# Q/k/v projection columns in blocks of 512 across head groups, with changed prices in the planner that orders the instructions

## The chip, the cores and the metric

The kernel runs on one NeuronCore of a Trainium2 chip. The metric is the device time of one execution in microseconds (us). The engines are named as in the profile: PE is the matrix engine and PEld its weight loads, DVE the vector engine, ACT the scalar engine, POOL the general engine, SP the engine that issues all DMAs of this kernel.

## What is computed

Two decoder layers over 1024 positions of 1024 features, all in float32. Each layer normalizes, projects to queries, keys, values and a gate, attends, multiplies by silu(gate) and projects back onto the residual. Layer A has 16 query heads and 2 key heads with a window of 128. Layer B has three groups (dilations 1, 4, 16) of 16 query heads and 4 key heads, merged by their softmax denominators. Cut to the part around the change:

```python
def mixer_b(h, w_in, q_gain, k_gain, cos, sin):
    z = h @ w_in
    heads = z[..., :N_GROUPS * B_GROUP_COLS].reshape(b, s, N_GROUPS, B_GROUP_COLS)
    gate = z[..., N_GROUPS * B_GROUP_COLS:]
    for g, (window, dilation) in enumerate(B_PAIRS):
        q, k, v = jnp.split(heads[:, :, g], [nq, nq + nk], axis=-1)
        q = partial_rope(rmsnorm(q...), cos, sin)
        k = partial_rope(rmsnorm(k...), cos, sin)
        o, lse = dilated_group(q, k, v, window, dilation)
    ...
    return o * jax.nn.silu(gate)
```

## The kernel before

Matrix products keep float32 accuracy by splitting each operand into a high and a low part and issuing three matmuls (`mm3`, L500): high by high, high by low, low by high. `load_w` (L452) loads a weight block in eight slices of 128 rows and splits each on ACT (high) and DVE (low) into the tile `wt`; there are 12 such tiles, so one block of eight and half of the next. `proj_tile` (L505) multiplies one tile of 128 positions by such a block: 24 matmuls into the PSUM tile `psz`, which ACT copies to `z`. `bounce` (L709) does this for the eight position tiles and writes each `z` to DRAM (`za`, `zb`); `fetch` (L716) reads the rows back as `zi`, in the order that the dilation wants.

Layer A is done in four passes `n` of four query heads: columns 384, 256, 384, 256 (a pair of passes shares its key head, whose columns go with the first). Layer B has four passes `n`, and in each the groups `g` = 2, 1, 0, each with a block of 384 columns (256 of queries, 64 of keys, 64 of values). A block is projected, and then eight attention units follow, one for each 128 positions. A unit is `prep` (L548) and `attend` (L594): on PE first two transposes of `zi` into `pq`, then one of the keys `kk` (in layer A in every second pass only), then the scores `pss`, the transposed probabilities `ptt` and the output `po`; between them stand DVE and ACT steps (`qs`, `kring`, `pe`, `pp`, `oh`). `gate_block` (L523) computes the gate into `psg` once in a pass. After group 0 a merge (`merge_b`, L937) goes through DRAM with the factors (`cr` to `cd` to `cb`). The output projections go into `psw`.

The order in which the engines get their instructions is not the order of the code. Every call is recorded in `Plan` (L98) with its dependencies and with a price from `_price` (L299): how long it occupies its engine, and after how long its result is there. `forward` (L209) is a list scheduler over the five engines; `issue` (L283) runs it with the code's order, then eight rounds with priorities from a backward pass, and emits the order with the shortest planned end. On the chip each engine then works through its own list in order, and an instruction whose operand is late holds what is behind it. In the plan a DMA occupies SP for `ISSUE` (475 ns), its data starts 1100 ns later, and it has landed `TRIP` (1900 ns) after that.

In `prep` the queries are split in two halves of 64 partitions: for each half ACT writes the high part into `qs[:HD, :, two]`, and DVE the low part into `qs[HD:, :, two]`, which reads ACT's result. The two halves' columns alternate in `qs`, in runs of 128.

Of the kernel before, what the change touches and what calls it, by code (L numbers as in the profile page):

```python
# [12 lines left out]
F32 = mybir.dt.float32  # L13
# [5 lines left out]
P = 128  # L19
# [30 lines left out]
TRIP = 1900  # L50
# [3 lines left out]
YB = 0  # L54
NB = {"pz": 2, "pS": 2, "pT": 2, "pO": 1, "pM": 1}
# [42 lines left out]
class Plan:  # L98
# [12 lines left out]
    ISSUE = 475  # L111
# [97 lines left out]
    def forward(self, prio, users):  # L209
# [12 lines left out]
        while len(order) < n:  # L222
# [8 lines left out]
            if e == "SP":  # L231
                free[e] = s + self.ISSUE
                wait = max(0.0, dma - s - 1100)
                dma = max(dma, s + 1100) + occ
# [64 lines left out]
def _price(eng, name, out, ins, kw):  # L299

    n = out.free_size()
    if eng == "SP":
        t = out.size() * 4 / 300.0
        return t, t + 1100 + TRIP
# [5 lines left out]
    accum = kw.get("accum_out") is not None  # L310
    if eng == "ACT":
        t = 70 + 0.84 * n + (70 if held else 0) + (0 if ins[0].space == bass.MemoryType.PSUM else 65)
        return (t + 93, t + 73) if accum else (t, t + 90)
    if eng == "DVE":
        if name == "tensor_reduce":
            last = ins[0].ap[-1][0]
            t = 75 + (1.04 if last == 1 else 1.78) * ins[0].free_size()
        elif name == "reciprocal":
            t = 100 + 8 * n
        elif name == "tensor_scalar":  # L320
            t = 130 + 0.53 * n
        else:
            wide = 2.1 if steps and min(steps) >= 4 and n >= 2 * P else 1.04
            t = 70 + wide * n
            t += 80 if name in ("tensor_tensor_reduce", "scalar_tensor_tensor") else 0
        return t, t + 75
    if kw.get("op") is OP.pow:
        t = 270 + 172 * n
    elif n <= 8:
        t = 300  # L330
    else:
        t = 1.95 * n if n > 512 else (50 if 200 < n < 400 else 160) + 2.1 * n
# [24 lines left out]
def trunk(ctx, tc, x, norm_a, w_in_a, q_gain_a, k_gain_a, sinks_a, w_out_a,  # L357
# [147 lines left out]
    def proj_tile(hT, t, w, width, r=None):  # L505
# [5 lines left out]
        z = nc.tile(sp, [P, 384], F32, tag="z", bufs=3, name="z")  # L511
# [36 lines left out]
    def prep(kind, order, tpos, z, nh, kv, slot):  # L548
# [160 lines left out]
    def bounce(hT, w, width, name, r=None):  # L709
        zd = tc.dram_tile([T, width], F32, name=name)  # L710
        for t in range(NT):
# [14 lines left out]
    def w_a(n, big=None):  # L726
        return load_w(w_in_a, (0, 384, 640, 1024)[n], 256 if n % 2 else 384, 0, big=big)
# [32 lines left out]

    def w_b(g, n, ks=range(NK)):
        return load_w(w_in_b, g * GCOLS + n * 384, 384, 1, ks)
# [27 lines left out]
    def out_a_whole(ts):  # L790
# [9 lines left out]
        w = w_b(2, 0, range(4))  # L800
# [8 lines left out]
        return w + w_b(2, 0, range(4, NK))  # L809
# [3 lines left out]
    for n in range(4):  # L813
        w = w_a(n, None if n else nc.tile(sp, [P, 4, 512], F32, tag="v0", bufs=1, name="wbig"))
# [4 lines left out]
        if n == 0:  # L819
            zd = tc.dram_tile([T, width], F32, name="za0")  # L820
            for t in range(NT):
# [19 lines left out]
                z = proj_tile(hT, t, w, width, ra)  # L841
                nc.sync.dma_start(zd[t * P:(t + 1) * P], z[:, :width])
# [10 lines left out]
        else:  # L853
            zd = bounce(hT, w, width, f"za{n}", ra)
# [39 lines left out]
    w0 = out_a_whole((6, 7))  # L894
# [168 lines left out]
```

## Time and profile before

| | |
|---|---|
| median of 3 runs | 1289.74 us (1287.47 to 1290.97) |
| the profiled execution | 1286.87 us, its span 1285.0 us |
| PE, PEld | 97%, 88% of the span |
| DVE, ACT, POOL | 80%, 69%, 55% |
| matmuls | 7851, of them 3072 into `psz` |
| DMA | 149.74 MB, mean 117 GB/s |

The span is the profile's time from the first to the last instruction; about 1.9 us lie outside it. Busy time on PE contains the overlap of pipelined matmuls, so that a busy share of 97% does not say how much of it is waiting for the issue of the next; the distance of matmuls that follow each other without a gap tells that.

### The profile page before, as it was taken

How to read it: one execution, taken by the hardware profiler on the slowest of the kernel's cores; microseconds unless marked ns; L12 is line 12 of the kernel's file. 1: busy time of each engine (PE TensorE's matmuls, PEld its weight loads, DVE VectorE, ACT ScalarE, POOL GpSimd, SP SyncE). 2: the span in 40 equal slices, each digit the busy share in tenths (PEclk: the TensorE clock that was granted, in tenths of full speed). 3: DMA queues.
4: the chain of work that ended last, by engine and by line, in shares of the span. 5: the costliest groups of instructions: out<-in, count | busy, mean ns of one | idle time of the engine just before them, and what ended most of it. 6: DMA issues, size and time to landing. Idle time of an engine off the chain costs nothing. (4 is left out here: it accounts for less than half of the span.)

```text
span 1285.0 us, 25754 instructions
## 1 busy us (share of the span) xinstructions
PE 1244.5 (97%) x7851; PEld 1136.3 (88%) x7851; DVE 1028.3 (80%) x2968; ACT 880.5 (69%) x2377; POOL 708.3 (55%) x1388
## 2 busy tenths in 40 slices
PE   7999999999999999999999999999999999999998
PEld 6999899998688999989888999988999988998776
DVE  8668888777955428878888878889888989779896
ACT  5367686877733437877767887767887766987661
POOL 5655455455500038556567655477656567786632
PEclk9999999999999999999999999999999999999999
DMA  6423223245444233223233323244233244454525
GB/s 226 141 76 103 84 80 117 81 146 178 123 129 140 99 104 99 81 71 111 93 125 122 91 73 111 88 139 135 79 95 91 94 130 128 140 174 129 173 80 181
DMA packets 142666, 149.74 MB, mean 117 GB/s; under 512 B 33576, under 2 KB 129344, under 8 KB 142528
## 3 DMA queue, kind: packets, MB, share of 16 engines
q1 hardware_dynamic: 142528, 148.09, 36.7%
q8 instruction: 63, 1.03, 0.3%
q14 instruction: 75, 0.61, 0.2%
HBM read 105.57 MB, written 42.47 MB: 115 GB/s over the span
## 5 line engine op out<-in xcount | busy, mean ns | idle before, releaser
L352 PE MATMUL psz<-wt,hT 128*128 128x384 f32 (+1 forms) x3072 | 632.9, 343 | 5.7 <-DVE wt L352 2.8
L352 PEld LDWEIGHTS psz<-wt,hT 128*128 128x128 f32 x3072 | 510.8, 190 | 16.2 <-DVE wt L352 3.6
L352 PE MATMUL psg<-hT,wt 128*128 128x256 f32 x1536 | 220.3, 291 | 0.3 <-DVE gT L352 0.3
L352 PEld LDWEIGHTS psg<-hT,wt 128*128 128x128 f32 x1536 | 200.3, 191 | 2.3 <-PE psg L352 0.5
L352 ACT ACTIVATE pe<-pe,st 128x128 f32<-128x128 f32 (+1 forms) x384 | 169.1, 442 | 36.2 <-DVE st L352 33.7
L352 PE MATMUL ptt<-ident,pe 128*128 128x128 f32 x800 | 170.8, 275 | 2.8 <-ACT pe L352 2.6
L352 DVE SCALAR_TENSOR_TENSOR qs<-pq,gt,qs 64x256 fp32r<-64x256 f32 x256 | 123.9, 484 | 44.8 <-ACT qs L352 38.5
L352 DVE TENSOR_TENSOR pp<-ptt,pp 128x512 fp32r<-128x512 f32 x200 | 131.5, 684 | 32.2 <-ACT pp L352 30.6
L352 POOL TENSOR_TENSOR r<-r,ex 128x5 f32<-128x5 f32 (+1 forms) x128 | 150.6, 1176 | 5.6
L352 ACT ACTIVATE qs<-pq,gt 64x256 fp32r<-64x256 f32 x256 | 120.1, 469 | 42.9 <-PE pq L352 36.2
L352 DVE SCALAR_TENSOR_TENSOR wt<-raw,gt,wt 128x384 fp32r<-128x384 f32 (+1 forms) x188 | 114.5, 639 | 28.5 <-ACT wt L352 26.6
L352 ACT ACTIVATE pp<-ptt 128x512 fp32r<-128x512 f32 x200 | 111.9, 595 | 35.9 <-PE ptt L352 35.1
L352 ACT ACTIVATE oh<-po 64x512 f32<-64x512 f32 x128 | 76.0, 594 | 82.2 <-PE po L352 78.5
L352 DVE CUSTOM_DVE_ANT_0 pe<-pss,con,r 128x256 f32<-128x256 f32 x288 | 123.5, 477 | 8.9 <-PE pss L352 8.5
L352 PEld LDWEIGHTS ptt<-ident,pe 128*128 128x128 f32 x800 | 105.7, 140 | 21.8 <-ACT pe L352 9.8
L352 ACT ACTIVATE wt<-raw,gt 128x384 fp32r<-128x384 f32 (+1 forms) x188 | 98.9, 564 | 19.6 <-DMA raw<-in_w_in_b_dram 6.9
L352 PE MATMUL po<-pp,vring 128*128 128x512 f32 x280 | 106.9, 416 | 3.8 <-ACT pp L352 1.5
L352 POOL TENSOR_SCALAR r<-ss 128x5 f32<-128x5 f32 (+1 forms) x128 | 30.3, 237 | 144.7 <-DVE st L352 55.5
L352 PE MATMUL psw<-hT,wy 128*128 128x512 f32 x384 | 107.8, 408 | 2.0 <-ACT wy L352 1.2
L352 POOL TENSOR_TENSOR sq<-zi 128x320 f32<-128x320 f32 (+1 forms) x128 | 93.8, 733 | 25.3 <-DMA zi<-za 9.8
L352 PE MATMUL pss<-kring,qs 128*128 128x256 f32 x560 | 99.3, 286 | 2.5 <-DVE kring L352 2.3
L352 POOL TENSOR_TENSOR t<-zi,rg 128x80 f32<-128x80 f32 (+1 forms) x128 | 48.4, 378 | 93.3 <-DMA zi<-zb 60.2
(142 smaller groups left out, 2175.3 us busy)
## 6 DMA issues: line engine op xcount, KB each, us to landing
raw<-in_w_in_b_dram SPq DMA_DIRECT2D x96, 192.0 KB
zb<-z SPq DMA_DIRECT2D x96, 192.0 KB
cb<-cd SPq DMA_DIRECT2D x128, 128.0 KB
zi<-zb SPq DMA_DIRECT2D x64, 192.0 KB
raw<-in_w_in_a_dram SPq DMA_DIRECT2D x48, 128.0 KB
yraw<-yd SPq DMA_DIRECT2D x24, 256.0 KB
zi<-zb SPq DMA_DIRECT2D x64, 96.0 KB
xt<-in_xt_dram SPq DMA_DIRECT2D x16, 256.0 KB
```

What stands on the lines that cost most here:

```text
L352: self.plan.add(self.name, method, lambda: fn(*args, **kw), outs, ins, price, func)
```

## The change

- **Blocks of columns.** The weights of layer B are laid out on the host in the order in which the program uses them, and a new class `Bounce` cuts the q/k/v columns of a layer into blocks that no longer end with a head group: in layer A 512, 512, 256 in place of 384, 256, 384, 256, in layer B six blocks of 512 and then four of 384 in place of twelve of 384. A block's `z` is written to one DRAM tensor for each group that it touches, so with one or two DMAs. A call for a group projects blocks until that group is covered.
- **Prices.** `TRIP` goes from 1900 to 2900 ns, `ISSUE` from 475 to 520, and several DVE, ACT and POOL prices change.
- **Query split.** `qs` is laid out half by half, so that a half's columns are contiguous. Both ACT copies are recorded first, and both DVE subtractions are given a dependency on the second of them in the plan.

```diff
-TRIP = 1900
+LEAD = 1100
+TRIP = 2900
+CUTA = (512, 1024, 1280)
+CUTB = [512, 1024, 1536, 2048, 2560, 3072, 3456, 3840, 4224, 4608]
...
-    for g in range(3):
-        for n in range(4):
+    for n in range(4):
+        for g in (2, 1, 0):
...
-    ISSUE = 475
+    ISSUE = 520
...
     if eng == "ACT":
-        t = 70 + 0.84 * n + (70 if held else 0) + (0 if ins[0].space == bass.MemoryType.PSUM else 65)
-        return (t + 93, t + 73) if accum else (t, t + 90)
+        if accum:
+            return 342 + 0.625 * n, 284 + 0.84 * n
+        t = 70 + 0.84 * n + (70 if held else 0) + (0 if psum else min(75, 0.4 * n) + 25 * held)
+        return t, t + 90
...
+        elif n <= 16:
+            return 105, 215
         else:
-            wide = 2.1 if steps and min(steps) >= 4 and n >= 2 * P else 1.04
-            t = 70 + wide * n
-            t += 80 if name in ("tensor_tensor_reduce", "scalar_tensor_tensor") else 0
-        return t, t + 75
+            t = 70 + 1.04 * n
+            if name in ("tensor_tensor_reduce", "scalar_tensor_tensor"):
+                t += 60 if psum else 105
+            elif steps and min(steps) >= 4:
+                return (70 + 1.82 * n, 145 + 1.82 * n) if n >= 2 * P else (70 + 1.18 * n, 220 + 1.18 * n)
+        return t, t + 78
...
-        z = nc.tile(sp, [P, 384], F32, tag="z", bufs=3, name="z")
+        z = nc.tile(sp, [P, 512], F32, tag="z", bufs=3, name="z")
...
-        qs = nc.tile(sp, [P, 2, 2, P], F32R, tag="qs", bufs=2, name="qs")
+        qs = nc.tile(sp, [P, 2, 2, P], F32R, tag="qs", bufs=2, name="qs").rearrange("p two pr q -> p pr two q")
         gq = gc[:, 0, kind:kind + 1]
         for two in range(2):
             rows = slice(two * HD, two * HD + HD)
             nc.scalar.activation(qs[:HD, :, two], pm[rows, 0:2], AF.Copy, scale=gq[rows])
+        nc.after = {nc.last["ACT"]}
+        for two in range(2):
+            rows = slice(two * HD, two * HD + HD)
             nc.vector.scalar_tensor_tensor(qs[HD:, :, two], pm[rows, 0:2], gq[rows], f(qs[:HD, :, two]),
                                            op0=OP.mult, op1=OP.subtract)
+        nc.after = set()
...
+        def tile(self, hT, t, w, o, width, r):
             z = proj_tile(hT, t, w, width, r)
-            nc.sync.dma_start(zd[t * P:(t + 1) * P], z[:, :width])
-        return zd
+            for end, wd, zd in zip(self.ends, self.widths, self.zd):
+                a, b = max(o, end - wd), min(o + width, end)
+                if a < b:
+                    nc.sync.dma_start(zd[t * P:(t + 1) * P, a - end + wd:b - end + wd], z[:, a - o:b - o])
+
+        def blocks(self, i):
+            while self.done < self.ends[i]:
+                o, width = self.block()
+                if o not in self.weights:
+                    self.prefetch()
+                yield o, width, self.weights.pop(o)
+                self.done += width
+
+        def group(self, i, hT, r=None):
+            for o, width, w in self.blocks(i):
+                for t in range(NT):
+                    self.tile(hT, t, w, o, width, r)
+            return self.zd[i]
...
+    za = Bounce("za", (384, 256, 384, 256), CUTA, lambda o, width, big=None: load_w(w_in_a, o, width, 0, big=big))
+    zb = Bounce("zb", (384,) * 12, CUTB, lambda o, width, ks=range(NK): load_w(w_in_b, o, width, 1, ks))
...
-            zd = bounce(hT, w, width, f"za{n}", ra)
+            zd = za.group(n, hT, ra)
...
-            w = w0 if n == 0 and g == 2 else w_b(g, n)
-            zd = bounce(hT, w, 384, f"zb{g}_{n}")
+            zd = zb.group(3 * n + 2 - g, hT)
```

Three places in the order of the instructions. The first is PE at the start of layer B: `psz` is the first projected block, and the first `pq` is the first attention unit of the layer. Before:

```order
L352 MATMUL psz<-wt,hT 128x384 x9
L352 MATMUL pm<-ident,hn 128x128 x4
L352 MATMUL psz<-wt,hT 128x384 x173
L352 MATMUL pq<-ident,zi 128x128 x2
L352 MATMUL psz<-wt,hT 128x384 x12
L352 MATMUL pq<-ident,kk 128x128
L352 MATMUL psz<-wt,hT 128x384 x6
```

and now:

```order
L362 MATMUL psz<-wt,hT 128x512 x7
L362 MATMUL pm<-ident,hn 128x128 x4
L362 MATMUL psz<-wt,hT 128x512 x180
L362 MATMUL pq<-ident,zi 128x128 x2
L362 MATMUL psz<-wt,hT 128x512 x10
L362 MATMUL pq<-ident,kk 128x128
L362 MATMUL psz<-wt,hT 128x512 x5
```

About as many matmuls stand ahead of the first unit, but each has 512 columns in place of 384.

The second place is PE at the boundary of layer B's second and third pass, from the first transposes of the 49th unit of the layer on (the first of the third pass). Before:

```order
L352 MATMUL pss<-kring,qs 128x256 x7
L352 MATMUL pq<-ident,zi 128x128 x2
L352 MATMUL psz<-wt,hT 128x384 x5
L352 MATMUL ptt<-ident,pe 128x128 x2
L352 MATMUL psz<-wt,hT 128x384 x7
L352 MATMUL ptt<-ident,pe 128x128 x2
L352 MATMUL psz<-wt,hT 128x384 x4
L352 MATMUL ptt<-ident,pe 128x128 x2
L352 MATMUL psz<-wt,hT 128x384 x4
```

and now:

```order
L362 MATMUL pss<-kring,qs 128x256 x3
L362 MATMUL pq<-ident,zi 128x128 x2
L362 MATMUL pss<-kring,qs 128x256 x3
L362 MATMUL ptt<-ident,pe 128x128 x5
L362 MATMUL psg<-hT,wt 128x256 x25
L362 MATMUL pq<-ident,kk 128x128
L362 MATMUL po<-pp,vring 128x512
L362 MATMUL psg<-hT,wt 128x256 x4
L362 MATMUL po<-pp,vring 128x512
L362 MATMUL ptt<-ident,pe 128x128 x4
L362 MATMUL pss<-kring,qs 128x256 x4
```

The projection that stood between the steps of the units is gone from here; the gate of the second pass (`psg`) stands there, and some steps follow each other directly.

The third place is ACT in a unit of layer B, with the semaphores that an instruction waits for in brackets (names with DVE, PE or DMA in them are of those engines). Before:

```order
L352 ACTIVATE qs<-pq,gt 64x2x128 [waits PE_49]
L352 ACTIVATE pp<-ptt 128x512 [waits PE_49]
L352 ACTIVATE pp<-ptt 128x512 [waits PE_49,Activation_49]
L352 ACTIVATE qs<-pq,gt 64x2x128 [waits DVE_49]
L352 ACTIVATE wt<-raw,gt 128x384 [waits DMAHW2_49]
```

and now:

```order
L362 ACTIVATE pp<-ptt 128x512 [waits PE_49,Activation_49]
L362 ACTIVATE qs<-pq,gt 64x256 [waits PE_49]
L362 ACTIVATE qs<-pq,gt 64x256
L362 ACTIVATE vring<-zi 128x64 [waits DMAHW1_49,PE_49,Pool_49]
L362 ACTIVATE oh<-po 64x512 [waits PE_49,Activation_49]
```

The second query copy waited for DVE's subtraction in this unit (it does so in 16 of the 128 units); now the two copies come without a wait between them in every unit.

## Rows read from the trace of the kernel before

**Rows 1.** The page's first part: busy us, share of span, instructions

```profile
PE 1244.5 (97%) x7851; PEld 1136.3 (88%) x7851; DVE 1028.3 (80%) x2968; ACT 880.5 (69%) x2377; POOL 708.3 (55%) x1388
```

**Rows 2.** PE's groups by shape: count, busy us, mean ns, idle before and releasers

```profile
L352 PE MATMUL psz<-wt,hT 128*128 128x384 f32 x2688 | 577.3, 351 | 5.7 <-DVE wt L352 2.8 <-ACT wt L352 1.5 <-DVE qs L352 0.6
L352 PE MATMUL psg<-hT,wt 128*128 128x256 f32 x1536 | 220.3, 291 | 0.3 <-DVE gT L352 0.3
...
L352 PE MATMUL psw<-hT,wy 128*128 128x512 f32 x384 | 107.8, 408 | 2.0 <-ACT wy L352 1.2 <-DVE wx L352 0.8
```

**Rows 3.** Timeline of PE, long runs: start us, length us, what, idle before

```profile
55.06 5.88 PE L352 MATMUL psg<-hT,wt 128*128 128x256 f32 x47
...
440.61 0.60 PE L352 MATMUL pm<-ident,hn 128*128 128x128 f32 x4
...
445.11 25.21 PE L352 MATMUL psz<-wt,hT 128*128 128x384 f32 x144
...
1260.63 11.09 PE L352 MATMUL psw<-hT,wy 128*128 128x512 f32 x48
...
1275.35 5.95 PE L352 MATMUL psw<-hT,wy 128*128 128x512 f32 x24 [1.17 <-ACT wy L352]
```

**Rows 4.** Timeline of the start, DVE and then PE

```profile
11.01 2.77 DVE L352 SCALAR_TENSOR_TENSOR wt<-raw,gt,wt 128x384 fp32r<-128x384 f32 x2
13.71 1.14 DVE L352 SCALAR_TENSOR_TENSOR wt<-wbig,gt,wt 128x384 fp32r<-128x384 f32 x2
...
13.31 8.88 PE L352 MATMUL psz<-wt,hT 128*128 128x384 f32 x34 [2.42 <-DVE wt L352]
```

**Rows 5.** Windows: us, busy us of PE, PEld, DVE, ACT, POOL, clock, DMA, GB/s

```profile
0.00:32.00 32.00, 22.39 (x101) 20.74 (x101) 25.92 (x29) 16.46 (x29) 17.15 (x18) 1.00 0.67 227
...
475.20:1178.30 703.10, 689.24 (x4404) 639.10 (x4403) 604.28 (x1848) 540.82 (x1523) 460.91 (x939) 1.00 0.35 108
...
665.40:726.40 61.00, 59.21 (x416) 55.65 (x415) 55.62 (x177) 44.34 (x134) 43.17 (x84) 1.00 0.32 98
...
822.00:893.70 71.70, 68.46 (x438) 62.38 (x437) 65.40 (x201) 49.46 (x142) 50.52 (x89) 1.00 0.43 133
```

**Rows 6.** DVE's waits from 475.2 to 1178.3: us, times, longest

```profile
DVE qs L352 <- ACT qs L352: 23.9, 36, 2.2
DVE pp L352 <- ACT pp L352: 19.4, 26, 1.5
DVE pe L352 <- PE pss L352: 14.3, 30, 0.9
```

**Rows 7.** Waits of PE's weight loads, whole run: us, times, longest

```profile
PEld ptt L352 <- ACT pe L352: 9.8, 32, 1.0
PEld po L352 <- DVE pp L352: 8.0, 24, 1.0
...
PEld pss L352 <- DVE kring L352: 3.9, 8, 1.2
PEld pq L352 <- issue: 3.8, 12, 0.7
PEld pq L352 <- POOL r L352: 3.8, 4, 1.1
```

**Rows 8.** ACT's and DVE's groups by shape

```profile
L352 ACT ACT_TABLE_LOAD x29 | 37.2, 1283 | 1.2 <-PEq L1048 0.7
...
L352 DVE SCALAR_TENSOR_TENSOR wt<-raw,gt,wt 128x384 fp32r<-128x384 f32 x108 | 70.4, 680 | 20.4 <-ACT wt L352 19.3
L352 DVE SCALAR_TENSOR_TENSOR wt<-raw,gt,wt 128x256 fp32r<-128x256 f32 x80 | 44.2, 583 | 8.1 <-ACT wt L352 7.2
```

**Rows 9.** Waits for landed DMAs, and issues of the read-back (min/median/max ns)

```profile
POOL t L352 <- DMA zi<-zb: 60.2, 18, 33.9
...
L352 SPq DMA_DIRECT2D zi<-zb x128: 319/460/1489, 465.5 to 1214.9; - x128
```

More of the change, by code (lines that the diff above doesn't have):

```diff
@@ L232, in forward @@
                 free[e] = s + self.ISSUE
-                wait = max(0.0, dma - s - 1100)
-                dma = max(dma, s + 1100) + occ
+                wait = max(0.0, dma - s - LEAD)
+                dma = max(dma, s + LEAD) + occ
             else:
@@ L303, in _price @@
         t = out.size() * 4 / 300.0
-        return t, t + 1100 + TRIP
+        return t, t + LEAD + TRIP
     if eng == "PE":
@@ L310, in _price @@
     accum = kw.get("accum_out") is not None
+    psum = bool(ins) and ins[0].space == bass.MemoryType.PSUM
     if eng == "ACT":
-        t = 70 + 0.84 * n + (70 if held else 0) + (0 if ins[0].space == bass.MemoryType.PSUM else 65)
-        return (t + 93, t + 73) if accum else (t, t + 90)
+        if accum:
+            return 342 + 0.625 * n, 284 + 0.84 * n
+        t = 70 + 0.84 * n + (70 if held else 0) + (0 if psum else min(75, 0.4 * n) + 25 * held)
+        return t, t + 90
     if eng == "DVE":
         if name == "tensor_reduce":
-            last = ins[0].ap[-1][0]
-            t = 75 + (1.04 if last == 1 else 1.78) * ins[0].free_size()
-        elif name == "reciprocal":
+            t = 80 + (1.04 if ins[0].ap[-1][0] == 1 else 1.78) * ins[0].free_size()
+            return t, t + 65
+        if name == "reciprocal":
             t = 100 + 8 * n
@@ L321, in _price @@
             t = 130 + 0.53 * n
-        else:
-            wide = 2.1 if steps and min(steps) >= 4 and n >= 2 * P else 1.04
-            t = 70 + wide * n
-            t += 80 if name in ("tensor_tensor_reduce", "scalar_tensor_tensor") else 0
-        return t, t + 75
+        elif n <= 16:
+            return 105, 215
+        else:
+            t = 70 + 1.04 * n
[4 more added lines that the diff above has]
+        return t, t + 78
     if kw.get("op") is OP.pow:
         t = 270 + 172 * n
-    elif n <= 8:
-        t = 300
+    elif name == "tensor_scalar":
+        return 300 + 1.25 * n, 235 + 1.35 * n
     else:
@@ L707, in out_first, with __init__, block, prefetch @@
         nc.bias = 0
-    def bounce(hT, w, width, name, r=None):
-        zd = tc.dram_tile([T, width], F32, name=name)
-        for t in range(NT):
-            z = proj_tile(hT, t, w, width, r)
-            nc.sync.dma_start(zd[t * P:(t + 1) * P], z[:, :width])
-        return zd
+    class Bounce:
+        def __init__(self, name, widths, cuts, load):
+            self.ends = list(np.cumsum(widths))
+            self.widths = widths
+            self.zd = [tc.dram_tile([T, w], F32, name=f"{name}{i}") for i, w in enumerate(widths)]
+            self.load, self.done, self.cuts = load, 0, cuts
+            self.weights = {}
+        def block(self):
+            return self.done, next(c for c in self.cuts if c > self.done) - self.done
+        def prefetch(self, **kw):
+            o, width = self.block()
+            self.weights[o] = self.weights.get(o, []) + self.load(o, width, **kw)
+        def tile(self, hT, t, w, o, width, r):
+            z = proj_tile(hT, t, w, width, r)
+            for end, wd, zd in zip(self.ends, self.widths, self.zd):
[4 more added lines that the diff above has]
+            while self.done < self.ends[i]:
+                o, width = self.block()
+                if o not in self.weights:
[7 more added lines that the diff above has]
+            return self.zd[i]
     def fetch(zd, width, rows):
@@ L724, in trunk @@
     hB = {}
-    def w_a(n, big=None):
-        return load_w(w_in_a, (0, 384, 640, 1024)[n], 256 if n % 2 else 384, 0, big=big)
+    za = Bounce("za", (384, 256, 384, 256), CUTA, lambda o, width, big=None: load_w(w_in_a, o, width, 0, big=big))
+    zb = Bounce("zb", (384,) * 12, CUTB, lambda o, width, ks=range(NK): load_w(w_in_b, o, width, 1, ks))
     def put_w(raw, w, k, half, hi, lo, sub):
@@ L759, in load_wout_b @@
         nc.bias = 0
-    def w_b(g, n, ks=range(NK)):
-        return load_w(w_in_b, g * GCOLS + n * 384, 384, 1, ks)
     def halves(a):
@@ L799, in out_a_whole @@
             got.append((t, x1, ps))
-        w = w_b(2, 0, range(4))
+        zb.prefetch(ks=range(4))
         nc.bias = -SECB
@@ L808, in out_a_whole @@
         nc.bias = 0
-        return w + w_b(2, 0, range(4, NK))
+        zb.prefetch(ks=range(4, NK))
     wo = {}
@@ L813, in trunk @@
     for n in range(4):
-        w = w_a(n, None if n else nc.tile(sp, [P, 4, 512], F32, tag="v0", bufs=1, name="wbig"))
+        if n == 0:
+            za.prefetch(big=nc.tile(sp, [P, 4, 512], F32, tag="v0", bufs=1, name="wbig"))
         if n % 2 == 0:
@@ L819, in trunk @@
         if n == 0:
-            zd = tc.dram_tile([T, width], F32, name="za0")
+            zd = za.zd[0]
+            (o, zw, w), = za.blocks(0)
             for t in range(NT):
@@ L840, in trunk @@
                     late_constants()
-                z = proj_tile(hT, t, w, width, ra)
-                nc.sync.dma_start(zd[t * P:(t + 1) * P], z[:, :width])
+                za.tile(hT, t, w, o, zw, ra)
             pr = nc.tile(pM, [P, 4, P], F32, tag="m", bufs=NB["pM"], name="pr")
@@ L893, in trunk @@
         norm_pair(j, [parts[2 * j + i] for i in range(2)])
-    w0 = out_a_whole((6, 7))
+    out_a_whole((6, 7))
     hT = hB
```

## Prediction

> **What bounds the kernel now.** I read the shares of the engines first [rows 1]: PE 97%, DVE 80%, ACT 69%. Since matmuls overlap, the 97% says only that PE nearly always has something in flight; how long a matmul holds the next one up is read from long runs of one kind [rows 3]. There I take off the last matmul's own duration (the means in [rows 2]; 0.27 us for a transpose) and divide by the steps: 144 of 384 columns give (25.21 - 0.35) / 143 = 173.9 ns, 48 of 512 give (11.09 - 0.41) / 47 = 227.2 ns, 47 of 256 give (5.88 - 0.29) / 46 = 121.5 ns, four transposes (0.60 - 0.27) / 3 = 110 ns.
>
> With these distances the stretch from the first attention unit of layer B to its 89th, 475.2 to 1178.3 us, can be taken apart. In the order PE has there 2036 projections of 384 columns (354.1 us), 768 gate matmuls (93.3), 500 scores (60.8), 330 of 512 columns (75.0) and 768 transposes (84.5): 667.7 us of work in 703.1 us. So PE is the bound, and it waits about 35 us in this stretch. The weight-load waits show for what [rows 7]: many waits of 0.3 to 1 us for a step of the attention chain that came a little late. DVE is the next engine: 604.3 of 703.1 us, 85.9% [rows 5], and up to 91% in parts of it (55.62 of 61.00, and 65.40 of 71.70 us). Time can thus come from less work on PE, or from fewer of these waits.
>
> **Part 1, wider blocks on PE.** From 384 to 512 columns a matmul gets 53.3 ns longer, 0.416 ns a column; what is left of 227.2 ns is 14 ns that every matmul costs whatever its width. Before, the projections are 2688 x 173.9 + 384 x 121.5 ns = 514.1 us. After, they are 1536 of 512 columns, 768 of 384 and 192 of 256: 349.0 + 133.6 + 23.3 = 505.9 us. That is 576 matmuls less and **-8.2 us**, on the engine that is the bound. The other end is the run of 24 that ends the kernel [rows 3]: (5.95 - 0.41) / 23 = 241 ns, by which the wide blocks would cost 13 us more than the old ones. I take the run of 48, since the projections run undisturbed for as long at the start of layer B.
>
> A rule speaks against this term. The Trainium skill (TensorE: Matmul & The Clock Gate, section "Back-to-back issue gap") gives the distance as the columns at 2.4 GHz plus 2.5 ns; by that an estimate of the gain is 576 x 2.5 ns = 1.4 us in place of 8.2. The rows disagree: the granted clock is 1.00, so 2.4 GHz, in the windows [rows 5], and the 512-column run is 13.9 ns over its columns' 213.3 ns, so I go by the rows.
>
> **Part 2, the start.** PE's first long run begins at 13.31 us, after a wait of 2.42 us for DVE's splits of the first weights [rows 4]. The eight slices are now 512 wide. DVE takes 680 ns for 384 columns and 583 for 256 [rows 8], so 97 ns for 128 columns, and 8 x 97 ns = 0.8 us more; the extra half megabyte takes 2.3 us at the 227 GB/s of this window [rows 5]. Between 0.8 and 2.3 I take **+1 us**, near the low end, since the transfers run beside the splits.
>
> **Part 3, where the work lies.** Ahead of the first unit of layer B PE has 652 projections of 384 and 384 of 256 columns before (160.0 us), and 645 of 512 and 192 of 256 now (169.9 us). So the units begin about 10 us later; nothing is lost by that while PE is busy, but those 10 us no longer fill gaps between the units. The order shows where it gets thin: a block of 512 covers a group and a third of the next, and around the third pass the projection has run ahead and its filler is missing. From the 45th to the 53rd unit of the layer, 822.0 to 893.7 us before, PE had 203 projections of 384 columns and 81 gate matmuls as filler (45.1 us), and now has 37 of 512 and 192 gate matmuls (31.7 us), 13.4 us less. With the units' own 79 transposes, 48 scores and 24 outputs (20.0 us) the work there was 65.1 of 71.7 us; now it is about 51 us. DVE was busy 65.4 us of these 71.7 [rows 5]; it has fourteen weight splits there before and eight now, 3.6 us less, so 61.8 us. At 91% busy, the most that it reaches, that takes 67.8 us, and PE waits 16.7 us in place of 6.6: 10.1 us more. Could DVE be full, it would be 4.1 us more. I take **+7 us**.
>
> **Part 4, the query split.** DVE waits 23.9 us for the first query copies in the stretch [rows 6], a quarter of its 98.8 idle us there. The planner of before did not know it: it let a subtraction start after the copy of its own half, while on the chip it followed both copies, or the second copy followed it. If PE's 35 us of waits follow DVE's idle time, a quarter of them is 8.6 us; if something else is late next (the subtractions `pp` after their ACT copies, 19.4 us, or the scores, 14.3 us, also in [rows 6]), nothing. I take **-5 us**.
>
> **Part 5, the other prices and the longer DMAs.** A read-back planned at a longer trip gets more work placed ahead of the unit that needs it. POOL waited for landed `zi` 18 times [rows 9], one of them the 33.9 us before layer B; the other 17 are 26.3 us. What reaches PE of it is in the waits ahead of `pq` (3.8 for POOL, 3.8 without a visible cause) and `kring` (3.9) [rows 7], 11.5 us at most, part of which Part 4 also claims. Between 0 and 8 I take **-3 us**. The planner may also do worse by an over-long trip: the merges then get filler that they don't need.
>
> **Edits that I cost at nothing.** SP issues 942 DMAs in place of 926: 40 more writes of `z`, 24 fewer weight loads. The second write of a `z` tile is queued on SP behind the first, one issue or 0.46 us [rows 9]; the read-backs of that group are what waits, covered by the PE work of the next block. Bare at eight block ends it would be 3.7 us. ACT makes 24 fewer weight splits, 24 fewer copies of `z` and four fewer table loads (4 x 1283 ns = 5.1 us) [rows 8]; ACT is not the bound, so 0, at best -2.
>
> **The sum.** -8.2 + 1 + 7 - 5 - 3 = -8.2 us against the profiled execution of 1286.9 us: 1278.7. That execution is 2.9 us under the median of the runs, so for the median I say 1281.5 us.
>
> **The rivals.**
> - *DVE becomes the bound of layer B's units; slower.* One mechanism: the units start 10 us later, and if DVE cannot get over the 85.9% that it has in the stretch, the stretch cannot get shorter than its DVE work. In layer B 96 splits of 384 columns (65.3 us) become 48 of 512 at 680 + 97 ns and 32 of 384 (59.1 us); some 5 us of the difference lie in the stretch, 6 us of time. Then the end moves by 9.9 + 1 - 6 = +5 us: 1295. It decides from the point at which PE's work per unit falls below DVE's, which Part 3 shows for eight of 96 units. Against it: two places of the trace with DVE at 91%.
> - *The new plan hands the gain back; no change.* PE does 8.2 us less, and the in-order queues meet as many late operands as before plus those of the thin place: -8.2 + 1 + 7 = 0, so 1287 to 1290. For it: most waits in [rows 7] are for `pe` and `pp`, whose prices hardly move.
> - *The fixed cost per matmul stays.* If a matmul's 14 ns were not saved with it, Part 1 falls to between 0 and 1.4 us and the sum to -1.4 or more: 1288. The issue-gap rule above would give this; the three distances in [rows 3] lie on one line with 14 ns left over, so I give it little.
>
> **How the numbers follow.** My forecast 0.6, DVE bound 0.2, handed back 0.17, fixed cost stays 0.03. A measurement of this kernel can tell about 0.3%, 3.9 us, from no change, so faster means under 1285.9 and slower over 1293.6. That makes 0.6 faster, 0.2 the same, 0.2 slower. The best ends of all parts (-8.2 + 0.8 + 4.1 - 8.6 - 8 - 2) give -22 us, 1268; with the thin place costing nothing, 1264. The worst without the 241 ns (-8.2 + 2.3 + 10.1 + 3.7) give +8 us, 1298. I take 1266 to 1297; the 241 ns, which would add 21 us, is left out.
>
> **What would show it.** In the profile after: 7275 matmuls, 576 fewer; a long run of 512-column `psz` at 227 ns from one to the next; PE's first long run about a microsecond later; the first unit of layer B some 10 us later; DVE's wait for `qs` well under 24 us; and a hole in PE's work with DVE over 90% around the third pass. I am wrong if DVE's share over layer B's units stays at 86% with PE's waits risen by 10 us or more (the first rival), or if PE's waits fall far under 35 us there and the thin place costs nothing, in which case the time is in the 1260s.

## The result, and the profile after

The changed kernel takes 1270.49 us (median of 4 runs, 1269.68 to 1271.92) beside 1288.61 us for the kernel before (1286.4 to 1290.97): a ratio of 0.986, 95% interval 0.984 to 0.988, so 18 us or 1.4% faster. The forecast was 1281.5. The sign came out as written; the gain is more than twice the one summed. The profiled executions differ by 14.9 us (1286.87 and 1271.92; the first is 1.7 us under its kernel's median, the second 1.4 over), and the accounts below are made between these two.

The first part of the page after, and its line of the granted clock over 40 slices; they answer to [rows 1]:

```profile
PE 1233.0 (97%) x7275; PEld 1068.3 (84%) x7275; DVE 1017.4 (80%) x2944; ACT 867.0 (68%) x2325; POOL 713.5 (56%) x1388
...
PEclk9999999999999999999999999999899999999999
```

There are 576 matmuls less, and the shares stand where they stood. One slice has an 8 in the clock; it returns in the last section. PE's groups by shape (count, busy us, mean ns, idle before), which answer to [rows 2]:

```profile
L362 PE MATMUL psz<-wt,hT 128*128 128x512 f32 x1536 | 419.9, 410 | 4.9 <-ACT wt L362 4.5 <-DVE wt L362 0.4
L362 PE MATMUL psg<-hT,wt 128*128 128x256 f32 x1536 | 223.2, 290 | 0.0
...
L362 PE MATMUL psz<-wt,hT 128*128 128x384 f32 x768 | 168.0, 353 | 0.0
```

PE's timeline at the start and at the first unit of layer B (start us, length us, what, how many, idle before), which answers to [rows 3, 4]:

```profile
12.31 10.40 PE L362 MATMUL psz<-wt,hT 128*128 128x512 f32 x34 [2.17 <-ACT wt L362]
...
439.93 41.09 PE L362 MATMUL psz<-wt,hT 128*128 128x512 f32 x180
480.85 0.38 PE L362 MATMUL pq<-ident,zi 128*128 128x128 f32 x2
```

The run of 180 has (41.09 - 0.41) / 179 = 227.3 ns from one matmul to the next, the 227.2 of the forecast.

Windows after (us, busy us of PE, PEld, DVE, ACT, POOL, granted clock, DMA share, GB/s): the stretch from the first to the 89th unit of layer B, and then three neighbouring stretches of four units each, the 45th to the 56th of the layer (here and below such rows begin up to 0.7 us after the first transposes of the unit named); they answer to [rows 5]:

```profile
481.50:1172.20 690.70, 678.33 (x4063) 594.47 (x4061) 597.01 (x1837) 531.39 (x1493) 463.45 (x937) 0.99 0.37 111
829.60:859.40 29.80, 28.21 (x190) 24.95 (x189) 28.79 (x92) 22.90 (x64) 16.60 (x28) 1.00 0.38 121
859.40:890.30 30.90, 26.25 (x190) 23.64 (x188) 29.79 (x92) 20.76 (x63) 28.94 (x49) 0.95 0.40 121
890.30:924.70 34.40, 32.38 (x179) 29.98 (x179) 30.18 (x96) 31.13 (x78) 23.98 (x51) 0.89 0.33 101
```

In the second and third row DVE is busy 96 to 97% of the time and PE has holes: this is the thin place that the prediction looked for. DVE's waits in the stretch of the first row (us, times, longest), which answer to [rows 6], and POOL's for landed read-backs over the whole run, as in [rows 9]:

```profile
DVE pp L362 <- ACT pp L362: 25.7, 33, 1.6
DVE pe L362 <- PE pss L362: 18.3, 30, 1.4
...
DVE qs L362 <- ACT qs L362: 10.8, 14, 3.5
```

```profile
POOL t L362 <- DMA zi<-zb: 51.3, 6, 43.6
```

DVE's wait for `qs` fell from 23.9 to 10.8 us, while `pp` and `pe` rose by 10.3 us together. POOL waits 6 times for a landed `zi` in place of 18; without the longest, 7.7 us in place of 26.3.

**PE's account.** With the distances of the prediction (110, 121.5, 173.9 and 227.2 ns for 128, 256, 384 and 512 columns) times the counts of the order I get PE's work in each stretch; the rest of the stretch is wait, and what a slower clock costs is in it too. The stretches: to the first score matmul `pss` of layer A, to the first of layer B, to the 741st `pss` of the program (near the end of layer B's units), to the last matmul.

| us | work in all | wait: start | layer A | layer B | end | in all |
|---|---|---|---|---|---|---|
| before | 1203.6 | 17.5 | 15.7 | 35.4 | 9.1 | 77.7 |
| after | 1195.3 | 19.0 | 9.9 | 33.1 | 9.1 | 71.1 |

So 8.3 us of the gain are work, 6.6 us are waits. The work is the counts times the distances, so its fall is measured only as far as the distances are. By groups of four units the waits of the 45th to the 56th unit of layer B rose from 6.9 to 15.6 us, and those of the rest of the layer's first 88 units fell from about 28.5 to 17.7.

### The profile page after: what moved, and what is told of

Same layout as the page of the kernel before. It is cut to its first block, busy times and chain, and to the rows that moved or that the text cites. A ratio compares the mean times of both kernels' runs of the same rounds, so it can differ in the third digit from the quotient of the medians.

```text
span 1270.1 us, 24500 instructions
## 1 busy us (share of the span) xinstructions
PE 1233.0 (97%) x7275; PEld 1068.3 (84%) x7275; DVE 1017.4 (80%) x2944; ACT 867.0 (68%) x2325; POOL 713.5 (56%) x1388
## 3 DMA queue, kind: packets, MB, share of 16 engines
q1 hardware_dynamic: 144832, 148.10, 37.4%
## 4 chain that ended last, share of the span: by engine, by line
PE 63%; DVE 8%; ACT 4%; issue 2%; DMA 2%; POOL 1%; SPq 0%; POOLq 0%; ACTq 0%; DVEq 0%
PE psz L362 29%; PE psw L362 12%; PE po L362 5%; PE pss L362 5%; PE ptt L362 5%; PE psg L362 4%; PE pq L362 2%; DVE pe L362 2%; ACT pe L362 1%; DMA cb<-cd 1%; DVE qs L362 1%; DVE og L362 1%; DVE pp L362 1%; DVE o L362 1%; DVE wt L362 1%
## 5 line engine op out<-in xcount | busy, mean ns | idle before, releaser
L362 PE MATMUL psz<-wt,hT 128*128 128x512 f32 (+2 forms) x2496 | 616.4, 383 | 4.9 <-ACT wt L362 4.5
L362 PEld LDWEIGHTS psz<-wt,hT 128*128 128x128 f32 x2496 | 435.6, 191 | 62.6 <-ACT wt L362 4.8
L362 PE MATMUL psg<-hT,wt 128*128 128x256 f32 x1536 | 223.2, 290 | 0.0
L362 ACT ACTIVATE pe<-pe,st 128x128 f32<-128x128 f32 (+1 forms) x384 | 169.0, 442 | 37.4 <-DVE st L362 34.1
L362 DVE SCALAR_TENSOR_TENSOR qs<-pq,gt,qs 64x256 fp32r<-64x256 f32 x256 | 123.8, 483 | 22.0 <-ACT qs L362 14.9
L362 POOL TENSOR_SCALAR r<-ss 128x5 f32<-128x5 f32 (+1 forms) x128 | 33.4, 261 | 190.7 <-DVE ss L362 119.1
L362 PEld LDWEIGHTS ptt<-ident,pe 128*128 128x128 f32 x800 | 105.3, 141 | 31.8 <-ACT pe L362 13.7
L362 DVE SCALAR_TENSOR_TENSOR wt<-raw,gt,wt 128x256 fp32r<-128x256 f32 (+2 forms) x164 | 105.2, 670 | 32.2 <-ACT wt L362 31.3
L362 ACT ACTIVATE wt<-raw,gt 128x256 fp32r<-128x256 f32 (+2 forms) x164 | 93.3, 603 | 20.7 <-PE psw L362 10.7
L362 PEld LDWEIGHTS pss<-kring,qs 128*128 128x128 f32 x560 | 85.4, 189 | 11.5 <-ACT kring L362 1.9
```

The lines of the kernel that those rows point to most:

```text
L362: self.plan.add(self.name, method, lambda: fn(*args, **kw), outs, ins, price, func)
```

## The experiments

All variants are the changed program with some of its parts set back; the class `Bounce` and the layout of the weights stay, and with the old cuts they give the old blocks. "Old blocks" means these two lines:

```diff
-CUTA = (512, 1024, 1280)
-CUTB = [512, 1024, 1536, 2048, 2560, 3072, 3456, 3840, 4224, 4608]
+CUTA = (384, 640, 1024, 1280)
+CUTB = [384 * (i + 1) for i in range(12)]
```

"Old trip" is `TRIP = 1900` and `ISSUE = 475`; "old prices" is the old `_price` for DVE, ACT and POOL; "old query" is:

```diff
-        qs = nc.tile(sp, [P, 2, 2, P], F32R, tag="qs", bufs=2, name="qs").rearrange("p two pr q -> p pr two q")
+        qs = nc.tile(sp, [P, 2, 2, P], F32R, tag="qs", bufs=2, name="qs")
...
-        nc.after = {nc.last["ACT"]}
-        for two in range(2):
-            rows = slice(two * HD, two * HD + HD)
...
-        nc.after = set()
```

The theory at the outset was that of the prediction: the wide blocks take 8 us of work off PE and pay most of it back at the thin place; the rest comes from the query split and the prices, in shares to be found. The rival: the parts matter little by themselves, and what moves is the luck of the new order.

### Each part alone, and the change without its blocks

**Blocks alone**: old trip, old prices, old query.

> Only the blocks of columns are changed; prices, DMA times and the query split are those of before. Truer plan (my theory): the waits of PE outside the thin place fell because the planner knows the chip better, so the blocks alone give their 8.2 us of PE work back to the later start and the thin place (-8.2 + 2 + 8): 1286 to 1291 us, with PE's waits at 78 us or more in all. Lighter blocks (rival): the waits fell because ACT and DVE have 48 and 24 instructions less, so the blocks alone give nearly all of the 18 us: 1270 to 1276 us, with PE's waits near 72 us.

Measured: 1279.93 us, ratio 0.9919 (0.9895 to 0.9943), so -10.7 us, between the two ranges. In its trace PE's work is 1195.3 us and its waits are 82.5, 4.8 more than before.

**Query split alone**: old blocks, old trip, old prices.

> Only the layout of the query tile and its recorded order and dependency are changed; blocks of 384 and all prices as before. Truer plan: -3 to -9 us, 1280 to 1286, DVE's wait for the query copies falls from 38.5 us to 20 or less, and PE's work is unchanged. Lighter blocks: within 3 us of before. Any new plan moves the time by some us either way (third theory): no link between DVE's wait for the query copies and the time.

Measured: 1276.26 us, 0.9887 (0.986 to 0.9915), -14.4 us, more than either theory had. Waits 63.8 us.

**Prices and trip alone**: old blocks, old query.

> Only the planner's prices, the longer DMA trip and the longer issue are changed; blocks of 384 and the query split as before. Truer plan: -5 to -10 us, 1279 to 1284, with fewer waits of PE for steps of the attention chain. Lighter blocks: within 3 us of before. Any new plan: anything from -6 to +6.

Measured: 1272.52 us, 0.9855 (0.9832 to 0.9877), -18.2 us, more than any of the theories had. Waits 66.1 us.

**Everything but the blocks**: old blocks only.

> The changed kernel with blocks of 384 and 256 columns as before: prices, DMA times and query split are the new ones, PE has all 7851 matmuls. Truer plan: -12 to -17 us, 1272 to 1277, layer A's and layer B's waits of PE down by about 6 and 11 us and no thin place in the third pass. Lighter blocks: 1285 to 1290.

Measured: **1260.51 us**, 0.9765 (0.9746 to 0.9784). This beats both kernels, by 30.2 and 10 us, and lies far under both ranges; that the lighter blocks carry the gain is out. Its work is the old 1203.6 us; its waits are 51.8 us, 25.9 under before. Its page, and its windows of the 45th to the 56th unit of layer B and of the first 88 units (columns as above):

```profile
PE 1230.9 (98%) x7851; PEld 1134.2 (90%) x7851; DVE 1021.7 (81%) x2968; ACT 874.2 (69%) x2373; POOL 709.7 (56%) x1388
```

```profile
808.80:846.30 37.50, 36.71 (x229) 33.94 (x228) 32.29 (x103) 24.94 (x70) 26.64 (x48) 1.00 0.40 124
846.30:878.80 32.50, 32.50 (x244) 31.64 (x243) 28.43 (x94) 22.92 (x68) 24.91 (x42) 1.00 0.48 144
878.80:908.10 29.30, 29.30 (x200) 28.15 (x199) 27.41 (x90) 27.73 (x76) 19.74 (x44) 1.00 0.30 92
...
470.60:1156.50 685.90, 680.52 (x4400) 638.52 (x4399) 597.03 (x1845) 538.87 (x1521) 457.06 (x931) 1.00 0.37 112
```

Where the changed kernel is thin, this one has 229, 244 and 200 matmuls in place of 190, 190 and 179, PE is never idle in two of the three rows, and its waits there are 2.2 us in place of 15.6. The last row settles one rival of the prediction: DVE does 597.0 us of work in 685.9 us, 87.0%, the work for which the changed kernel takes 690.7 us. So the 85.9% of before [rows 5] was no bound.

### How much is the luck of an order?

Two kernels whose order was made anew by a constant that means nothing, then the trip alone, and another first block.

**The kernel before's parts with TRIP 1910** in place of 1900:

> The kernel before with one number of the planner changed by next to nothing: the DMA trip from 1900 to 1910 ns. The instructions are the same, their order is planned anew. Truer plan: the time stays within 4 us of before, since the planner knows no more than it did. Luck of the plan (rival since the runs with one part each all gained 10 to 18 us): the order of before is a bad draw, and this one is 8 us or more faster.

Measured: 1282.76 us, 0.9947 (0.9932 to 0.9962): -6.9 us for nothing, between the 4 and the 8 of the two theories.

**The changed kernel with TRIP 2910** in place of 2900:

> The changed kernel with the DMA trip at 2910 in place of 2900 ns. Truer plan: within 4 us of the changed kernel, 1266 to 1275, the thin place with its waits of about 15 us is still in the third pass, since the blocks make it. Luck of the plan: anywhere from 1262 to 1283, and the thin place may be gone.

Measured: 1269.53 us, 0.9839 (0.9825 to 0.9854), 1 us under the changed kernel. Its thin place is there too (14.3 us of waits in the 45th to the 56th unit).

**Trip and issue alone**: old blocks, old query, old prices, `TRIP = 2900`, `ISSUE = 520`.

> The kernel before with the DMA trip at 2900 and the issue at 520 ns, all other prices, the blocks and the query split as before. Truer plan with the trip as its main part: 1275 to 1281, most of what the prices and the trip gain together (1272.5). Truer plan with the other prices as its main part: 1284 to 1290. Luck of the plan: no telling.

Measured: 1281.54 us, 0.9938 (0.992 to 0.9956). That is 8.1 us under before and 1.2 us under the draw of TRIP 1910, so by itself the long trip is worth no more than a draw; the time lies between the ranges of the first two theories. Yet its trace shows POOL's waits for landed `zi` almost gone but for the one at the head of layer B:

```profile
POOL t L355 <- DMA zi<-zb: 39.5, 4, 35.6
```

**A first block of 384 columns**, so that layer B's units can start earlier:

```diff
-CUTB = [512, 1024, 1536, 2048, 2560, 3072, 3456, 3840, 4224, 4608]
+CUTB = [384, 896, 1408, 1920, 2432, 2944, 3456, 3840, 4224, 4608]
```

> The changed kernel with layer B's cuts shifted: one block of 384 first, six of 512, then four of 384, so ten blocks and the same work on PE. The first unit of layer B then starts with the first block of 384, some 10 us earlier. If the late start and what it leaves unfilled is what the blocks cost, 1260 to 1266, with the first unit near 472 us and PE's waits under 62 us. If it is the uneven filler wherever the cuts lie, 1267 to 1275, with a thin place at another unit.

Measured: 1272.08 us, 0.9855 (0.9839 to 0.9871), the time of the changed kernel within a draw. The first unit starts at 473.6 us, 7.2 us earlier, and nothing comes of it: two other thin places (the units 29 to 32 and 77 to 80 of the layer) wait 5.8 and 8.9 us.

### Moving the thin place

**Cuts with the same number of wide blocks, two of the 384 in the middle**, so that projections are left for the third pass:

```diff
-CUTB = [512, 1024, 1536, 2048, 2560, 3072, 3456, 3840, 4224, 4608]
+CUTB = [512, 1024, 1536, 1920, 2304, 2816, 3328, 3840, 4224, 4608]
```

> The changed kernel with layer B's cuts at 512, 1024, 1536, 1920, 2304, 2816, 3328, 3840, 4224, 4608: ten blocks and the same PE work, but the groups without a block of their own (the fourth and the tenth) now both stand first in their pass, and the eighth, before whose units the thin place was, has its own. If the thin place is what the blocks cost over the same planner without them (1260.5), its 13 us of waits go and the time is 1256 to 1263. If uneven filler costs wherever it lies, 1266 to 1274, with waits of 10 us or more at other units of layer B.

Measured: 1261.62 us, 0.9777 (0.9756 to 0.9798), 9 us under the changed kernel with the same work on PE (1195.3 us). Two of its three windows over the same units:

```profile
857.80:887.60 29.80, 29.80 (x180) 25.49 (x179) 27.11 (x88) 21.90 (x66) 21.07 (x38) 1.00 0.49 145
887.60:924.80 37.20, 36.52 (x247) 32.97 (x246) 30.63 (x95) 30.71 (x78) 25.25 (x51) 1.00 0.36 104
```

The waits of the 45th to the 56th unit are 2.5 us in place of 15.6. But its 1261.6 is also the time of the kernel without any wide block (1260.5): 8.3 us less work and 59.9 us of waits in place of 51.8. The waits that came back are not in one place: 0.7 us more at the start, 0.9 in layer A, 5.1 in layer B, 1.4 at the end.

**The same, with layer A's old blocks** (`CUTA = (384, 640, 1024, 1280)`):

> As the run with the moved cuts, but layer A's blocks are those of before (384, 256, 384, 256). PE has 192 matmuls more, 2.7 us of work. If the wider first block of layer A costs its 2 to 3 us at the start and in layer A as the two traces say, the same time within 3 us; if layer A's blocks cost more than they give, 3 to 6 us faster.

Measured: 1261.33 us, 0.9776 (0.9757 to 0.9796). Layer A's wide blocks bring nothing.

**Everything but the blocks, with TRIP 2910**, a second draw of the best kernel:

> Prices, longer DMAs and query split with the blocks of before, and the DMA trip at 2910 in place of 2900 ns. Truer plan: within 4 us of 1260.5. Luck of the plan: that kernel is a good draw as the one before was a bad one, and this one is 5 us or more slower.

Measured: 1264.48 us, 0.9794 (0.9773 to 0.9815), 4 us over the first draw and still 6 us under the changed kernel.

**The engines' prices alone**: old blocks, old query, old trip.

> The kernel before with the new prices of ACT, DVE and POOL alone: trip 1900 and issue 475 ns, blocks and query split as before. If the prices of the engines carry what prices and trip gain together, 1270 to 1276; if they carry no more than another draw of the plan does (1282.8 in the run that moved the trip by 10 ns), 1279 to 1286.

Measured: 1275.73 us, 0.9882 (0.9863 to 0.9901), -14.9 us.

### Which draws hold, and what the trip is worth

**The kernel before's parts with ISSUE 478** in place of 475:

> The kernel before with the issue at 478 in place of 475 ns, nothing else. If the order of before is a bad draw, 1279 to 1286 again, as with the trip moved by 10 ns (1282.8); if that run was itself the lucky one, 1287 to 1293.

Measured: 1288.11 us, 0.9972 (0.9953 to 0.9991), -2.7 us. So the kernel before is not an unlucky draw by much; the -6.9 of TRIP 1910 is the largest step for nothing that I saw. The run has the class `Bounce` and the new layout of the weights, so these do no more than 2.7 us by themselves, unless the draw hides it.

**Query split alone with TRIP 1910**:

> The query split of the change on the kernel before, as in the run with the query split alone (1276.3), with the trip at 1910 ns. If the query split is worth more than a draw, 1272 to 1280, under every draw of the old prices without it (1280 to 1290); if not, 1281 to 1290.

Measured: 1273.88 us, 0.9867 (0.9824 to 0.9911). With 1276.26 of the first draw, the split alone is worth 14 to 17 us. In its two traces PE waits 10.2 and 13.7 us in layer A (15.7 before) and 29.8 and 27.7 in layer B (35.4 before).

**Prices and query without the trip**: old blocks, old trip.

> New prices of ACT, DVE and POOL and the query split, blocks of before, trip 1900 and issue 475 ns as before. If the longer DMAs are worth no more than a draw, 1258 to 1266 beside 1260.5 and 1264.5 with them; if they carry a part of the gain, 1267 to 1274.

Measured: 1273.93 us, 0.9869 (0.9832 to 0.9906). Together the two give no more than either alone, and the long trip on top of them gives another 13.4 us (9.4 by the second draw).

**Moved cuts without the trip**: as the first of the kernels with moved cuts, old trip.

> The moved cuts with the new prices and query split, and the trip and issue of before. If the longer DMAs are worth no more than a draw, 1257 to 1266 beside 1261.6 with them; if wider blocks need the longer trip, since each of their weight loads is longer, 1267 or more.

Measured: 1274.84 us, 0.9875 (0.9837 to 0.9913): the trip is worth 13.2 us here too, as much as with the old blocks, so it is not the wider blocks that need it.

The pair with and without the trip (old blocks, new prices and query) in the trace: POOL's waits for `zi`, and the weight loads' wait for DVE's `pp` ahead of the output matmuls. Without:

```profile
POOL t L362 <- DMA zi<-zb: 51.7, 10, 32.8
```

```profile
PEld po L362 <- DVE pp L362: 13.5, 24, 1.8
```

With the long trip:

```profile
POOL t L362 <- DMA zi<-zb: 43.8, 7, 34.0
```

```profile
PEld po L362 <- DVE pp L362: 4.4, 12, 0.8
```

POOL waits 9.1 us less for landed read-backs in this row without the longest (18.9 to 9.8), and PE's visible gain stands in the row of `pp`, 9.1 us, not in rows of `pq`: those that wait for no visible cause were 2.1 us and are 5.2. That one led to the other is my reading of rows that moved together; the runs don't prove the link, and with the moved cuts, where the trip gains as much, the row of `pp` falls by 3.6 us only (8.0 to 4.4). PE's account says where the trip's gain lies: half of it or more is in layer A, whose waits fall from 16.3 to 8.4 us, and with the moved cuts from 20.5 to 9.3 (of the 20.5, 3.4 us or less are a clock of 0.50 for 6.8 us).

### The parts beside each other

| median us | old trip | long trip |
|---|---|---|
| old blocks | 1289.7; draws 1282.8, 1288.1 | 1281.5 |
| old blocks, query | 1276.3, 1273.9 | not run |
| old blocks, prices | 1275.7 | 1272.5 |
| old blocks, prices, query | 1273.9 | 1260.5, 1264.5 |
| wide blocks | 1279.9 | not run |
| wide blocks, prices, query | not run | 1270.5, 1269.5 |
| moved cuts, prices, query | 1274.8 | 1261.6, 1261.3 (layer A old) |

The first entry is the median of the prediction's runs; beside the other runs the same kernel took 1288.6 to 1290.9. Of the six pairs that differ only by a meaningless constant or by layer A's blocks, the steps are 0.3 to 6.9 us, so I read no difference under 7 us as an effect of a part.

## Why the prediction came out as it did

**Part 1 was right.** Forecast -8.2; the order has the 576 matmuls less, and the distance of the wide blocks, by which they save 8.3 us, is 227.3 ns in a run of 180. The other end of the bound, 241 ns from the run that ends the kernel, and with it 13 us, did not apply. By the formula of the Trainium skill (TensorE: Matmul & The Clock Gate, section "Back-to-back issue gap") an estimate of the distance is 215.8 ns; the section gives it for a matmul by itself and says that a stream of weight loads and matmuls keeps another, so the prediction read it too widely. The run of 180 does not agree with it. The third rival is out by the same run: a wide matmul has the same 14 ns over its columns as a narrow one, so each matmul less saves them.

**Part 2 is not borne out.** Forecast +1 us, found 1.5 us more wait at the start, but the clock makes that: it was halved there for 3.4 us, and 14 wide matmuls lost 1.6 us by it (last section). Four kernels with the same first blocks and no such drop (blocks alone, TRIP 2910, moved cuts with the long and the old trip) wait 16.8 to 18.1 us at the start, from 0.7 us under before to 0.6 over, all less than the low end of the forecast, 0.8. What I named as its sign was wrong too: PE's first long run begins at 12.31 us, a microsecond earlier than the 13.31 of [rows 4]. It holds about as much waiting as that one: its 34 matmuls take 10.40 us where 33 x 227.2 ns and the last one's 0.41 make 7.9, those of before 8.88 where 6.1 would do.

**Part 3 was right in place, and in size by luck.** Forecast +7 (4.1 to 10.1) for the 45th to the 52nd unit, because DVE would set the pace there. DVE did run nearly full, but the waits of these eight units rose by 3.2 us only (6.4 to 9.6): I took 91% as the most that DVE reaches, and it was busy 96 to 97%, and it had 58.6 us of work there in place of 61.8. The other 5.5 of the 8.7 us stand in the next four units, nearly all in the 53rd, which waits 4.9 us; DVE was as busy there, 7.8 of the first 7.9 us, and in these the clock was at 0.50, which I had not seen (last section). And one line ahead of the prediction was wrong: the gate matmuls that stand at the thin place are the third pass's own, not the second's. The first unit started 5.7 us later, not 10, since layer A's waits fell by 5.8.

**Parts 4 and 5 failed in size.** Forecast -8 together. In the profile the waits outside the thin place and the start fell by 5.8 (layer A) and 10.8 us (layer B), 16.6. Without the blocks, the two parts give 26 to 30 us (1260.5 and 1264.5 beside 1290.7 and 1290.6 of the kernel before next to them). Part 4 was read from layer B's stretch and Part 5 from layer B's read-backs (`zi<-zb`); layer A, whose queries are split and whose order is planned in the same way, stood in the sum with nothing. For the wait for `qs`, 23.9 us in layer B's stretch [rows 6], the whole run of before has this row (us, times, longest):

```profile
DVE qs L352 <- ACT qs L352: 38.5, 55, 4.6
```

Three steps of the working broke:

- *Part 4, the stretch.* The term was taken from layer B's first 88 units, and 14.6 us of the 38.5 lie outside them. In layer B the term held: alone, the split takes 5.6 and 7.7 us of waits from it, in two draws, beside the forecast's 5 and its end of 8.6. In all it was worth 14.4 and 17.0 us. That the wait for `qs` is what did it is not shown: with everything but the blocks DVE waits 12.8 us for it in the first 88 units of layer B, with the change 10.8, though the first kernel is 10 us faster.
- *Part 5, the cap.* I let the longer trip reach PE only through the waits ahead of `pq` and `kring` (11.5 us) and took 3 of it. That it empties POOL's waits was right: those for `zi` without the longest are 17 to 34 us in the nine traces with the short trip, and 2 to 10 us in eight of nine with the long one (19 us with the block of 384 first). But what it is worth depends on the rest of the plan: a draw by itself (1281.5 beside 1282.8), 9 to 13 us on top of prices and query, there with half or more of it in layer A.
- *Part 5, the prices.* The engines' prices, to which I gave no term of their own, were worth 15 us alone.

**The rivals.** *DVE becomes the bound* did not happen in the stretch as a whole. Its share stayed near 86% (597.0 of 690.7), as I had named for its sign, but PE's waits did not rise, and the kernel without the blocks reached 87.0% with the same DVE work. It is right at the thin place only. *The new plan hands the gain back* did not decide the result, but its mechanism is there: with new prices, query and trip, moved cuts against old blocks save 8.3 us of work and wait 8.1 us more. In the changed kernel the blocks even cost 5 to 10 us: 1270.5 and 1269.5 beside 1260.5 and 1264.5. That alone is at the edge of a draw; that it is the thin place is borne out by the moved cuts, 8 to 9 us faster at the same work in both draws. PE's account of the changed kernel against that with old blocks says where: -8.3 work, +1.6 at the start (the halved clock), +1.5 in layer A, +14.2 in layer B, +2.0 at the end, and 13.4 of the 14.2 are the thin place (15.6 beside 2.2 us). Without the blocks the other parts would have emptied that place as well, so it costs more than the 8.7 us that show against before.

**What made the prediction wrong** is thus not the part that the change is named for, but the -8 of Parts 4 and 5: waits that were read from a few rows of layer B, with layer A and the engines' prices at nothing, where 16.6 us went in the profile and 26 to 30 us without the blocks. Nor do these parts add: query -14 to -17, prices -15, both -17, both with the long trip -26 to -30. **Open** are why the query split gains what it gains, why prices and query together give no more than each alone while the trip is short, which of the prices matters, and whether 1260 us is near the least that this order-making can reach.

## What to carry to other kernels

Work taken off the bounding engine can be summed from distances and counts; waits could not be summed here from rows of waiting, and the parts measured alone did not add up either, so cost them by running each part alone and together. Give every stretch that a part touches a term, also the one that you did not look at. Where a planner makes the order, run the kernel once or twice with a constant moved by nothing, and believe no part worth less than that scatter (here up to 7 us of 1290). Filler of the bounding engine was here worth as much as its work: wider blocks save matmuls, but the ones saved are missing where the units have nothing else, so look for the place where the filler runs out, and move the cuts before giving up on them.

## What the runs showed of the hardware

I had not expected the clock to fall in a hole of a few microseconds. PE's timeline in the changed kernel's thin place:

```profile
885.72 0.30 PE L362 MATMUL pq<-ident,kk 128*128 128x128 f32 x1 [1.46 <-DVE qs L362]
887.46 1.25 PE L362 MATMUL ptt<-ident,pe 128*128 128x128 f32 x3 [1.45 <-ACT pe L362]
...
891.82 1.18 PE L362 MATMUL ptt<-ident,pe 128*128 128x128 f32 x4 [1.38 <-DVE pp L362]
...
894.17 1.48 PE L362 MATMUL psz<-wt,hT 128*128 128x384 f32 x4
895.45 0.41 PE L362 MATMUL pq<-ident,kk 128*128 128x128 f32 x1
895.52 3.60 PE L362 MATMUL psz<-wt,hT 128*128 128x384 f32 x14
```

And windows of it, two microseconds each, with the granted clock in the third column from the end:

```profile
886.00:888.00 2.00, 0.55 (x3) 0.33 (x2) 1.83 (x9) 1.45 (x7) 2.00 (x4) 0.82 0.64 212
888.00:890.00 2.00, 2.00 (x8) 1.64 (x9) 1.72 (x7) 1.69 (x6) 1.84 (x4) 0.50 0.21 53
...
892.00:894.00 2.00, 1.82 (x6) 1.23 (x6) 1.95 (x6) 1.95 (x6) 1.82 (x5) 0.50 0.38 131
894.00:896.00 2.00, 2.00 (x8) 1.81 (x8) 1.95 (x5) 1.26 (x4) 1.43 (x4) 0.50 0.18 50
896.00:898.00 2.00, 2.00 (x9) 2.00 (x8) 1.97 (x6) 1.98 (x5) 0.52 (x1) 0.62 0.48 148
898.00:900.00 2.00, 2.00 (x14) 1.91 (x13) 0.64 (x2) 1.96 (x3) 0.09 (x1) 1.00 0.66 195
```

The clock falls to 0.50 (1.2 GHz) at about 887.3 us, near the end of the second of two waits (1.46 and 1.45 us) with one transpose between them, and is back at about 897.5 us, 10.2 us later (both times worked out from the shares 0.82 and 0.62 of their windows). The four projections of 384 columns at 894.17 and the fourteen at 895.52 take 1.48 and 3.60 us, where 173.9 ns from one to the next and a last one of 0.35 make 0.87 and 2.61: 1.6 us lost in these two alone. The short steps of the units take longer too (the `kk` transpose at 895.45 takes 0.41 us, the one at 885.72 0.30); that the thin place feeds itself in this way, its late operands coming later still, is my reading, which no run separates. The kernel with a first block of 384 shows the same in its own thin place, from about 1083.4 us for 6.8 us:

```profile
1083.00:1086.00 3.00, 1.97 (x6) 1.27 (x7) 2.97 (x13) 2.95 (x12) 2.82 (x5) 0.57 0.43 148
1086.00:1089.00 3.00, 3.00 (x11) 2.81 (x10) 2.89 (x9) 1.97 (x5) 1.95 (x5) 0.50 0.25 75
1089.00:1092.00 3.00, 3.00 (x15) 2.91 (x15) 1.20 (x3) 2.41 (x3) 0.64 (x1) 0.79 0.44 116
```

The changed kernel has one more such drop, at the start: the clock is at 0.50 from about 37.4 us for 3.4 us, behind a wait of 2.67 us, and the first of two equal runs takes 1.6 us longer than the second:

```profile
37.14 0.33 PE L362 MATMUL pr<-ident,sr 128*128 128x128 f32 x1 [2.67 <-DVE nss L362]
37.22 5.04 PE L362 MATMUL psz<-wt,hT 128*128 128x512 f32 x14
...
42.13 3.45 PE L362 MATMUL psz<-wt,hT 128*128 128x512 f32 x14
```

```profile
36.00:40.00 4.00, 2.86 (x8) 2.31 (x9) 4.00 (x5) 0.35 (x1) 1.83 (x4) 0.67 0.10 33
40.00:44.00 4.00, 4.00 (x18) 3.21 (x17) 4.00 (x5) 0.69 (x1) 2.41 (x3) 0.90 0.21 68
```

The kernel with moved cuts and that without wide blocks have none of this at these units (clock 1.00 in their windows above), and their mean clocks are 0.999 and 1.000, beside 0.994 for the changed kernel.
